# Turning keys, queries and values of the Delta heads and values of GLA in 32x32 blocks through DRAM, and moving beta into the decays

## Chip, cores and metric

One Trainium2 chip, one NeuronCore of it. The metric is device microseconds of one execution. The kernel before has a median of 978.31 us over three runs (978.17 to 978.34). The profile is one execution whose span, first to last instruction, is 976.7 us.

## What is computed

One inference step of two layers over 256 prompt tokens and 8 x 8 sample tokens, width 2048. Layer 0 mixes tokens with 8 gated Delta heads (128 x 128) and 4 GLA heads (128 x 256), layer 1 with an RG-LRU; each has one big projection in and one out. The change touches the two kinds of heads of layer 0. For a Delta head, with keys k and queries q of norm one, G the running sum of the decays and b the beta of a token:

```python
kb = k * beta[..., None]
A = jnp.where(strict, jnp.einsum('nbhid,nbhjd->nbhij', kb, k) * decay, 0.0)
rhs = jnp.concatenate([v * beta[..., None], kb * jnp.exp(G)[..., None]], axis=-1)
sol = lax.linalg.triangular_solve(A + jnp.eye(C, dtype=jnp.float32), rhs,
                                  left_side=True, lower=True, unit_diagonal=True)
qk = jnp.einsum('nbhid,nbhjd->nbhij', q, k) * decay
# per chunk, state S:
v_new = u_c - w_c @ S;  o = qg_c @ S + qk_c @ v_new
S = S * exp(g_last) + k_dec.T @ v_new
```

GLA needs, per chunk, the products of its scores and of its decayed keys with its values v.

## The kernel before

**The main stream.** The weights are cut into 30 groups of 512 columns with 8 chunks of 512 KB each. For a chunk TensorE (PE) runs 24 matmuls into acc (L380), each over 320 tokens: two rows of 128 inputs, four blocks of 128 columns, and three products, since weights and activations are split into a high and a low part (wh, wl; xh, xl). SP loads a chunk into one of three buffers wst (L212); ScalarE (ACT) makes wh (L246) and VectorE (DVE) wl (L247), six buffers of each, so three chunks. PE never leaves this stream by itself.

**The background.** All other work are Python generators, advanced one step per slot; a slot comes after each three acc matmuls. The table WAITS gives the number of slots that a generator lets pass at a named point. What results is one fixed order of instructions per engine; no engine reorders at run time. SP issues its DMAs in order too and has eight rotating lanes: a DMA waits until the DMA eight places ahead on its lane has landed. A wait of any instruction therefore holds all that stands behind it on its engine.

**Delta heads.** The projection leaves k, q and v with the head's dimension on partitions and tokens along the row. delta_half(0) and delta_half(1) each treat four heads over 256 tokens, as two quads (c = 0 and 1: four heads, 128 tokens); delta_sample treats the sample tokens as one more quad. In quad_a (L710) TensorE transposes k (kt, L716), q (qt, L725) and v (vt, L767) of the four heads; ACT copies the turned keys and squares keys and queries for the norms; the decays' matrix dtm comes from df (L751), gr from the same; kk (L773) times dtm is bt, kq (L785) times dtm is mt. nb is minus beta over the squared key norm; it is turned too (nbt, L795) and stored by POOL to nb_scratch. bt's diagonal 32 x 32 blocks go by SP to bd_scratch (L780).

**The inverse.** invert32 (L806) loads the blocks of eight heads' units with four DMAs into ab (L817) and nb into bn (L819), POOL multiplies the two (L823), runs 31 steps of two operations (L828, L830) and stores the inverse blocks to xd_scratch (L835). load_inv (L867) loads them as XT (L871) and, in other places, xc (L876). quad_front (L896) transposes xc into xz on DVE (L910, L920), multiplies blocks on PE (lp, L916; lxt, L926), and DVE scales lp by nb into xp (L907), which the next lxt reads. quad_b then makes y0, the outputs and the state. The sample's inverse runs on DVE (L838).

**GLA.** gla_head, per head and chunk, transposes two blocks of values (gvt, L1438) and the decayed keys (L1439) on PE; ACT copies the three.

Of the kernel before, what the change touches and what calls it, by code (L numbers as in the profile page):

```python
# [7 lines left out]
F32 = mybir.dt.float32  # L8
# [6 lines left out]
P = 128  # L15
# [57 lines left out]
def hybrid_step(ctx, tc, x_cols, x_rows, w_head, w_dense, w_small, w_lr, w_gate, par_a, par_b, par_c, gains, last_gain,  # L73
# [9 lines left out]
    nb_d = nc.dram_tensor("nb_scratch", (20, P), F32, kind="Internal").ap()  # L83
# [3 lines left out]
    xt_d = nc.dram_tensor("xt_scratch", (4, P, P), F32, kind="Internal").ap()  # L87

# [457 lines left out]

    def evac_conv_a(slot_name, half, part):
# [133 lines left out]
    def quad_prompt(half, c):  # L681
# [10 lines left out]
        q.late = c > 0  # L692
        q.on_tag, q.nbuf = "lg", 2
        return q

    def quad_sample():
# [9 lines left out]
        q.late = True  # L706
        q.on_tag, q.nbuf = "bt", 1
        return q

    def quad_a(q, ws, nbuf):  # L710
        U = q.U
        t = lambda nm, shape=[P, 4, P], bufs=nbuf, tag=None: ws.tile(shape, F32, name=nm, tag=tag or nm, bufs=bufs)
        ss = t("ss", [P, 8])
        ps = bank4("kt")
        for u in range(U):
            pe.transpose(ps[:, u, :], q.k(u), ident)  # L716
        q.ktm = t("ktm")
        act.activation(q.ktm, ps, AF.Copy)
        for u in range(U):
            j = t("junk", [P, P], 1)  # L720
            act.activation(j, ps[:, u, :], AF.Square, accum_out=ss[:, u:u + 1])
        yield from wait("quad_a.1")
        ps = bank4("qt")
        for u in range(U):
            pe.transpose(ps[:, u, :], q.q(u), ident)  # L725
        for u in range(U):
            j = t("junk", [P, P], 1)
            act.activation(j, ps[:, u, :], AF.Square, accum_out=ss[:, 4 + u:5 + u])
        q.bk = t("bk", [P, 4])
        q.nb = t("nb", [P, 4])  # L730
        q.nbe = t("nbe", [P, 4])
        sk = ss[:, 0:4]
        pool.tensor_scalar(sk, sk, EPS, None, op0=OP.add)
        pool.tensor_tensor(q.bk, sk, mhalf[:, :4], OP.pow)
        pool.tensor_mul(q.bk, q.bk, beta[:, q.gc:q.gc + 4])
# [8 lines left out]
        yield from wait("quad_a.2")  # L744
        dve.reciprocal(q.nb, sk)
        dve.scalar_tensor_tensor(q.nb, q.nb, -1.0, beta[:, q.gc:q.gc + 4], op0=OP.mult, op1=OP.mult)
# [13 lines left out]
        dve.tensor_mul(dt, dt, q.um[:, None, :].to_broadcast([P, 4, P]))  # L760
        q.eq = ss[:, 4:8]
        dve.tensor_scalar(q.eq, q.eq, EPS, EPS * P, op0=OP.add, op1=OP.mult)
        dve.tensor_mul(q.nbe, q.nb, es[:, q.gc:q.gc + 4])
        yield from wait("quad_a.3")
        ps = bank4("vt")
        for u in range(U):
            pe.transpose(ps[:, u, :], q.v(u), ident)  # L767
        q.rv = t("rv")
        scaled4(q.rv, ps, q.bk, NA0)
        yield from wait("quad_a.4")  # L770
# [5 lines left out]
        yield from wait("quad_a.5")  # L776
# [18 lines left out]
        pe.transpose(ps[:4, :P], q.nb, ident)  # L795
        nbt = t("nbt", [4, P], 1)
        act.activation(nbt, ps[:4, :P], AF.Copy)
        pool.dma_start(nb_d[q.id:q.id + 4, :], nbt)
        yield from wait("quad_a.7")
# [6 lines left out]
    def invert32(ws, first):  # L806
# [4 lines left out]
        bn = ws.tile([P, n], F32, name="bn", tag="bn")  # L811
# [7 lines left out]
        act.dma_start(bn, bass.AP(tensor=nb_d.tensor, offset=nb_d.offset + first * P, ap=[[0, 4], [n, 4 * U], [1, n]]))  # L819
# [3 lines left out]
        pool.tensor_mul(ab, ab, bn[:, None, :].to_broadcast([P, n, n]))  # L823
# [14 lines left out]
    def invert(ws, n_units, n):  # L838
# [4 lines left out]
        bn = ws.tile([parts, n], F32, name="bn", tag="bn")  # L843
# [5 lines left out]
        act.dma_start(bn[:parts], nb_d[16:16 + n_units].rearrange("u (b i) -> (u b) i", i=n))  # L849
# [3 lines left out]
        dve.tensor_mul(ab[:parts], ab[:parts], bn[:parts, None, :].to_broadcast([parts, n, n]))  # L853
# [42 lines left out]
    def quad_front(qs, x, x2, pt, xt, xc):  # L896
# [8 lines left out]
        def scale(ps, rows, w):  # L905
            for c, q in enumerate(qs):
                dve.tensor_mul(pt[c][rows, :, :w], ps[rows, 4 * c:4 * c + 4, :w],  # L907
# [1190 lines left out]
```

## Time and profile before

| what | value |
|---|---|
| median of three runs | 978.31 us |
| span of the profiled execution | 976.7 us |
| PE busy | 965.7 us (99%) |
| DVE, ACT, POOL busy | 695.6, 532.6, 193.4 us |
| granted TensorE clock, mean | 0.997 |
| busy share of the DMA queue of SP (q1) | 54.5% |
| packets under 512 B of all | 17116 of 68125 |
| half 0's quads, first kk to first lp on PE | 122.30 to 193.00 us |
| half 1's | 239.80 to 310.35 us |

The profiled execution has only its span; the runs' times are about 1.6 us above it. In rows of a timeline the columns are start, duration, engine, line, operation and tiles; "x4" means that several are shown as one row, whose duration runs from the first's start to the last's end. In the list of waits the columns are total, count and longest. A matmul's recorded duration is longer than its distance to the next, because PE pipelines them. SPq is SP's queue: its durations are those of issuing, not of the transfer.

### The profile page before, as it was taken

The page shows a single profiled execution, that of the slowest core. Times are in us where ns is not written, and L with a number is a line of the kernel's source. Part 1 is how long each engine was busy: PE and PEld are TensorE (multiplying, and loading weights), DVE is VectorE, ACT ScalarE, POOL GpSimd, SP SyncE. Part 2 cuts the span into 40 slices and gives each one's busy share as a digit, 9 for nine tenths or more (in the row PEclk, how much of TensorE's full clock was granted, in tenths as well). Part 3 has the DMA queues.
Part 4 walks back from the last instruction along what each step waited for, and adds up shares of the span by engine and source line. Part 5 has one row for each costly group of instructions (what it writes and reads, how often), then busy time and mean ns, then how long its engine had stood idle before and what let it go on. Part 6 is the DMA issues. An engine that isn't in the chain of part 4 may idle for free.

```text
span 976.7 us, 18827 instructions
## 1 busy us (share of the span) xinstructions
PE 965.7 (99%) x6945; PEld 949.2 (97%) x6945; DVE 695.6 (71%) x1464; ACT 532.6 (55%) x1088; POOL 193.4 (20%) x343
## 2 busy tenths in 40 slices
PE   9999999999999999999999999999999999999996
PEld 9999999999999999999989999999999999999996
DVE  7498887666545556788658789667969668876763
ACT  7666865447333454866423345348685885333442
POOL 3010128303381011120106124100010000042200
PEclk9999999999999999999999999999999999999998
DMA  9854445534455376444578887655445445678752
GB/s 321 292 176 123 134 131 155 166 109 121 150 154 150 98 235 215 130 125 130 180 251 265 245 246 249 211 154 151 157 117 189 131 127 171 189 229 253 264 168 108
DMA packets 68125, 175.06 MB, mean 179 GB/s; under 512 B 17116, under 2 KB 26096, under 8 KB 67520
## 3 DMA queue, kind: packets, MB, share of 16 engines
q1 hardware_dynamic: 62904, 163.69, 54.5%
q0 software_dynamic: 2720, 8.66, 2.5%
q10 hardware_dynamic: 2408, 1.49, 0.5%
q8 instruction: 55, 0.90, 0.4%
q14 instruction: 38, 0.31, 0.1%
HBM read 159.14 MB, written 14.68 MB: 178 GB/s over the span
## 4 chain that ended last, share of the span: by engine, by line
PE 96%; DVE 2%; issue 0%; DMA 0%; ACT 0%; SPq 0%; POOL 0%; DVEq 0%; ACTq 0%; POOLq 0%
PE acc L380 82%; PE acc L266 3%; PE fbt L309 1%; PE gpo L1495 0%; PE lg L1683 0%; PE lg L1682 0%; PE lg L1684 0%; PE kq L785 0%; PE kk L773 0%; DMA wst<-in_w_head_dram 0%; PE gsn L1259 0%; PE po L971 0%; PE pq L1059 0%; PE sn L1245 0%; PE y L962 0%
## 5 line engine op out<-in xcount | busy, mean ns | idle before, releaser
L380 PE MATMUL acc<-xh,wh 128*128 128x320 f32 x1856 | 579.9, 313 | 0.4 <-ACT wh L233 0.4
L380 PE MATMUL acc<-xl,wh 128*128 128x320 f32 x1856 | 574.0, 310 | 0.0
L380 PE MATMUL acc<-xh,wl 128*128 128x320 f32 x1856 | 573.0, 309 | 0.2 <-DVE wl L247 0.2
L246 ACT ACTIVATE wh<-wst 128x512 fp32r<-128x512 f32 x479 | 279.2, 624 | 301.1 <-PE acc L380 259.5
L247 DVE TENSOR_TENSOR wl<-wst,wh 128x512 fp32r<-128x512 f32 x479 | 333.4, 726 | 150.6 <-ACT wh L246 149.6
L380 PEld LDWEIGHTS acc<-xh,wh 128*128 128x128 f32 x1856 | 348.6, 188 | 3.3 <-issue 1.3
L380 PEld LDWEIGHTS acc<-xl,wh 128*128 128x128 f32 x1856 | 348.6, 188 | 1.1
L380 PEld LDWEIGHTS acc<-xh,wl 128*128 128x128 f32 x1856 | 348.2, 188 | 0.9 <-DVE wl L247 0.4
L588 DVE SCALAR_TENSOR_TENSOR yc<-slab,pa,yc 128x344 f32<-128x344 f32 x72 | 40.6, 576 | 2.8 <-ACT yc L102 2.4
L830 POOL TENSOR_TENSOR xi<-xi,tmp 128x60 f32<-128x60 f32 (+24 forms) x62 | 25.9, 418 | 4.9
L828 POOL TENSOR_TENSOR tmp<-ab,xi 128x60 f32<-128x60 f32 (+24 forms) x62 | 25.1, 404 | 4.8
L1711 POOL MEMSET aa<- 128x32 f32 x4 | 0.6, 161 | 117.7 <-ACT rr L1698 66.7
L1140 POOL TENSOR_TENSOR uvkh<-uvk,uvkh 32x256 fp32r<-32x256 f32 (+1 forms) x8 | 10.8, 1344 | 51.5 <-DVE uvkh L1136 50.6
L1249 DVE SCALAR_TENSOR_TENSOR ust<-ust,es,sn 128x128 f32<-128x128 f32 x64 | 18.2, 338 | 2.8 <-PE sn L1245 2.0
L1145 POOL TENSOR_TENSOR uvm<-uvh,rm 96x512 fp32r<-96x512 f32 x16 | 19.5, 1242 | 2.8 <-PE sn L1245 2.4
L885 POOL TENSOR_TENSOR so<-so,mhalf 128x4 f32<-128x4 f32 x4 | 4.4, 1106 | 74.2 <-DVE so L884 74.2
L266 PE MATMUL acc<-xl,wh 128*128 128x320 f32 (+1 forms) x64 | 18.7, 292 | 0.0
L266 PE MATMUL acc<-xh,wl 128*128 128x320 f32 (+1 forms) x64 | 18.7, 292 | 0.0
L266 PE MATMUL acc<-xh,wh 128*128 128x320 f32 (+1 forms) x64 | 18.6, 291 | 0.0
L592 ACT ACTIVATE qkv<-yc 128x256 f32<-128x256 f32 x24 | 10.0, 415 | 15.8 <-DVE yc L588 15.6
L1263 DVE SCALAR_TENSOR_TENSOR ugt<-ugt,ebs,gsn 128x256 f32<-128x256 f32 x32 | 14.1, 474 | 5.6 <-PE gsn L1259 5.5
L1642 DVE SCALAR_TENSOR_TENSOR yc<-slab,pb,yc 128x344 f32<-128x344 f32 x32 | 17.5, 572 | 0.6 <-ACT yc L1640 0.5
(464 smaller groups left out, 1057.1 us busy)
## 6 DMA issues: line engine op xcount, KB each, us to landing
wst<-in_w_dense_dram SPq DMA_DIRECT2D x237, 512.0 KB, 4.0
st<-in_state_delta_dram SPq DMA_DIRECT2D x8, 512.0 KB, 6.3
st<-in_state_gla_dram SPq DMA_DIRECT2D x4, 1024.0 KB, 6.9
ust<-in_state_delta_dram SPq DMA_DIRECT2D x8, 512.0 KB
out_s_delta_dram<-ust POOLq DMA_DIRECT2D x8, 512.0 KB, 5.1
ugt<-in_state_gla_dram SPq DMA_DIRECT2D x8, 512.0 KB, 5.6
out_s_gla_dram<-ugt POOLq DMA_DIRECT2D x8, 512.0 KB, 4.2
xtok<-in_x_rows_dram SPq DMA_DIRECT2D x6, 512.0 KB, 5.4
```

The costliest lines, as they stand in the source:

```text
L246: act.activation(h, wst[i][:, a, :], AF.Copy)
L247: env["last_split"] = dve.tensor_sub(l, wst[i][:, a, :], h.bitcast(F32))
L266: mm = pe.matmul(accs[f][:, cols], w[:, fs], x[:, cols], start=(k == 0 and j == 0), stop=(k == KT - 1 and j == 2), skip_group_check=True)
L380: mm = pe.matmul(o, (h, h, l)[j][:, fs], (xh, xl, xh)[j][k], start=(k == 0 and j == 0), stop=(k == KT - 1 and j == 2))
L588: dve.scalar_tensor_tensor(y[:, :n], xp[:, j:j + n], pa[:, ft, j:j + 1], y[:, :n], op0=OP.mult, op1=OP.add)
L828: behind(pool.tensor_mul(tv, ab[:, j, j + 1:, None].to_broadcast([P, m, w]), xi[:, j:j + 1, :w].to_broadcast([P, m, w])))
L830: behind(pool.tensor_add(xi[:, j + 1:, :w], xi[:, j + 1:, :w], tv))
L1140: pool.tensor_sub(o, t[rows, :, cols], o.bitcast(F32))
L1145: pool.tensor_mul(m, src.bitcast(F32)[:, None, :].to_broadcast([R, 4, P]), rm4[:R, :, None].to_broadcast([R, 4, P]))
L1249: dve.scalar_tensor_tensor(s_, s_, es[:, col:col + 1], ps[:, b, :], op0=OP.mult, op1=OP.add)
L1263: dve.scalar_tensor_tensor(s_, s_, ebs[:, h, 4 * hb + b + i:4 * hb + b + i + 1], ps[:, i * 256:(i + 1) * 256], op0=OP.mult, op1=OP.add)
L1642: dve.scalar_tensor_tensor(y[:, :n], xp[:, j:j + n], pb[:, ft, 2 + j:3 + j], y[:, :n], op0=OP.mult, op1=OP.add)
```

## The change

The turn is no longer made on PE. As soon as a column group has left k, q or v, turn (new) has DVE transpose its 32 x 32 blocks into a buffer of the layer (ob) and SP store that to tp_scratch (512 KB; 256 KB to ts_scratch for the sample). quad_a then loads each tensor with four strided DMAs of 128 x 128 (load_turned), which put the blocks where the whole transpose would have them: kin, qin and rv for kt, qt and vt. Which of the tensors is loaded late depends on the half (late): in half 0 the values, in half 1 the queries. GLA's values go the same way; its keys stay on PE. In the loaded values the 32-column blocks of a head are apart, so y0's and GLA's matmuls and some DVE operations read them in strides.

The rows of bt are scaled by nb while it is made: dtm is multiplied by nb and the mask in one operation per head. So nbt, its store, bn and POOL's multiplication of ab go, and lp is only copied into xp, by DVE for one quad and ACT for the other. v, eg and wv use other factors accordingly. quad_a's waits are moved, and quad_a.7 falls from 9 slots to 2.

```diff
-    "quad_a.4": 0, "quad_a.5": 0, "quad_a.6": 0, "quad_a.7": 9, "invert32.1": 18, "invert32.2": 13,
+    "quad_a.4": 0, "quad_a.5": 0, "quad_a.6": 0, "quad_a.7": 2, "invert32.1": 18, "invert32.2": 13,
...
+    def turn(src, d, flag, to, gate):
+        while gate not in env["done"]:
+            yield
...
+        for f in range(4):
+            behind(dve.transpose(out[:, f], src[:, f, :].rearrange("p (x j) -> p x j", j=32)))
+            yield from wait("turn.1")
+        yield from wait("turn.2")
+        behind(sp.dma_start(d, to))
+        env["done"].add(flag)
+        yield from wait("turn.3")
+
+    def load_turned(out, d, c=0):
+        w = d.shape[1]
+        for b in range(4):
+            sp.dma_start(out[32 * b:32 * b + 32].rearrange("p a u j -> p a (u j)"), bass.AP(
+                tensor=d.tensor, offset=d.offset + c * 4 * P + b * P, ap=[[w, 32], [32 * w, 4], [1, P]]))
...
     def quad_a(q, ws, nbuf):
-        ps = bank4("kt")
-        for u in range(U):
-            pe.transpose(ps[:, u, :], q.k(u), ident)
...
+        kin = rows("kin", "mt")
+        load_turned(kin, *turned(1))
+        late = {0: 2, 1: 0}.get(half)
+        if late != 0:
+            qin = rows("qin", "bt")
+            load_turned(qin, *turned(0))
+        if late != 2:
+            q.rv = rows("rv")
+            load_turned(q.rv, *turned(2))
...
-        dve.tensor_mul(dt, dt, q.um[:, None, :].to_broadcast([P, 4, P]))
...
+        for u in range(U):
+            j = t("junk", [P, P], 1)
+            act.activation(j, q.ktm[:, u, :], AF.Square, accum_out=ss[:, u:u + 1])
...
+        for u in range(U):
+            dve.scalar_tensor_tensor(dt[:, u, :], dt[:, u, :], q.nb[:, u:u + 1], q.um, op0=OP.mult, op1=OP.mult)
...
-        ps = bank("nbt")
-        pe.transpose(ps[:4, :P], q.nb, ident)
...
     def invert32(ws, first):
-        pool.tensor_mul(ab, ab, bn[:, None, :].to_broadcast([P, n, n]))
...
     def quad_front(qs, x, x2, pt, xt, xc):
-        def scale(ps, rows, w):
-            for c, q in enumerate(qs):
-                dve.tensor_mul(pt[c][rows, :, :w], ps[rows, 4 * c:4 * c + 4, :w],
-                               q.nb[rows, :, None].to_broadcast([rows.stop - rows.start, 4, w]))
+        def keep(ps, rows, w):
+            dve.tensor_copy(pt[0][rows, :, :w], ps[rows, 0:4, :w])
+            act.activation(pt[1][rows, :, :w], ps[rows, 4:8, :w], AF.Copy)
...
     def gla_head(h, ws, vt):
-            for hf in range(2):
-                pe.transpose(pt[:, hf, :], env["VB", vt // 4][:, vt % 4, cs], ident)
```

On PE the products of both quads of a half now stand in one block: kk, kq, kk, kq. In half 0 they come behind 744 acc matmuls (before: 726 and 730) and lp behind 1134 (before 1171); in half 1 behind 1350 (1383 and 1387) and 1740 (1827). Half 0 thus has 390 acc matmuls between the products and lp, where 441 stood between the second quad's products and lp; half 1 has 390 too, where 440 stood.

SP in half 0, from the blocks' stores on; bd_scratch are bt's diagonal blocks, ab their load for the inverse, wst a chunk of weights. Before:

```order
L780 DMA bd_scratch<-bt 32x4x32 x8
L212 DMA wst<-in_w_dense_dram 128x1024
L817 DMA ab<-bd_scratch 32x1024 x2
L520 DMA out_dconv_dram<-stc 128x108
L817 DMA ab<-bd_scratch 32x1024
L212 DMA wst<-in_w_dense_dram 128x1024
L817 DMA ab<-bd_scratch 32x1024
L212 DMA wst<-in_w_dense_dram 128x1024 x7
```

And after the change, where tp_scratch is the store of the turned values and rv their loads:

```order
L213 DMA wst<-in_w_dense_dram 128x1024 x3
L830 DMA bd_scratch<-bt 32x4x32 x8
L561 DMA tp_scratch<-ob_137 128x1024
L213 DMA wst<-in_w_dense_dram 128x1024
L880 DMA ab<-bd_scratch 32x1024
L569 DMA rv<-tp_scratch 32x4x128 x8
L880 DMA ab<-bd_scratch 32x1024 x3
L213 DMA wst<-in_w_dense_dram 128x1024 x2
L521 DMA out_dconv_dram<-stc 128x108
```

The eight loads of values and their store now stand between the blocks' stores and three of their four loads, and one chunk stands there, not two.

SP in half 1, before:

```order
L212 DMA wst<-in_w_dense_dram 128x1024 x10
L780 DMA bd_scratch<-bt 32x4x32 x8
L212 DMA wst<-in_w_dense_dram 128x1024
L817 DMA ab<-bd_scratch 32x1024
L212 DMA wst<-in_w_dense_dram 128x1024
L817 DMA ab<-bd_scratch 32x1024 x2
L212 DMA wst<-in_w_dense_dram 128x1024
L817 DMA ab<-bd_scratch 32x1024
```

and after, from the loads of the second quad's keys on (kin and qin are turned keys and queries):

```order
L569 DMA kin<-tp_scratch 32x4x128 x4
L569 DMA rv<-tp_scratch 32x4x128 x4
L213 DMA wst<-in_w_dense_dram 128x1024
L561 DMA tp_scratch<-ob_137 128x1024
L830 DMA bd_scratch<-bt 32x4x32 x8
L569 DMA qin<-tp_scratch 32x4x128 x4
L213 DMA wst<-in_w_dense_dram 128x1024 x2
L569 DMA qin<-tp_scratch 32x4x128 x4
L561 DMA ts_scratch<-ob_139 128x512
L213 DMA wst<-in_w_dense_dram 128x1024
L880 DMA ab<-bd_scratch 32x1024 x4
```

Between the blocks' stores and the first of their loads stand now eight loads of queries, a store of the sample's turned tensor and three chunks; a burst of sixteen loads (keys and values of two quads) stands ahead of one more chunk.

DVE where half 0's inverse comes back: xz are its blocks, turned from xc; xp is what the first lp leaves for lxt. Before:

```order
L247 TENSOR_TENSOR wl<-wst,wh 128x512
L588 SCALAR_TENSOR_TENSOR yc<-slab,pa,yc 128x344
L910 STREAM_TRANSPOSE xz<-xc 32x8x32 x2
L588 SCALAR_TENSOR_TENSOR yc<-slab,pa,yc 128x344
L247 TENSOR_TENSOR wl<-wst,wh 128x512
L588 SCALAR_TENSOR_TENSOR yc<-slab,pa,yc 128x344
L907 TENSOR_TENSOR xp<-lp,nb 32x4x32
L588 SCALAR_TENSOR_TENSOR yc<-slab,pa,yc 128x344
L907 TENSOR_TENSOR xp<-lp,nb 32x4x32 x3
```

and after, where ob are the sample's keys being turned:

```order
L967 STREAM_TRANSPOSE xz<-xc 32x8x32 x2
L977 STREAM_TRANSPOSE xz<-xc 32x8x32
L558 STREAM_TRANSPOSE ob_139<-smpK 128x4x32
L248 TENSOR_TENSOR wl<-wst,wh 128x512
L558 STREAM_TRANSPOSE ob_139<-smpK 128x4x32
L248 TENSOR_TENSOR wl<-wst,wh 128x512
L480 TENSOR_TENSOR slab<-acc,rb_84 128x256
L481 TENSOR_TENSOR slab<-acc,rb_84 128x8x8
L964 COPY xp<-lp 32x4x32
```

The first copy of lp now stands behind two more splits (wl) and two evacuations of acc into slab; before one split stood there.

More of the change, by code (lines that the diff above doesn't have):

```diff
@@ L606, in after @@
                 hi.append(later(lambda: lo.extend([delta_half(1), delta_sample()])))
+            if part or half:
+                turn_conv(part, half, ob[1], "x0")
+            if part == 1 and half == 0:
+                turn_conv(0, 0, ob[0], "x0")
+            if half:
+                turn_sample(part)
         evac.late = late
@@ L692, in quad_prompt @@
         q.late = c > 0
+        q.at = half, c
         q.on_tag, q.nbuf = "lg", 2
@@ L712, in quad_a @@
         t = lambda nm, shape=[P, 4, P], bufs=nbuf, tag=None: ws.tile(shape, F32, name=nm, tag=tag or nm, bufs=bufs)
+        half, c = q.at
+        turned = lambda part: (tp_d[2 * part + half], c) if q.n == 32 else (ts_d[part], 0)
         ss = t("ss", [P, 8])
-        ps = bank4("kt")
-        for u in range(U):
[L716 to L735, printed above, removed]
+        rows = lambda nm, tag=None: t(nm, [P, 4, 4, 32], tag=tag)
+        kin = rows("kin", "mt")
[7 more added lines that the diff above has]
+            load_turned(q.rv, *turned(2))
         if q.n == 32:
@@ L743, in quad_a @@
                            g.bitcast(F32)[:, q.gc:q.gc + 4, None].to_broadcast([P, 4, P]))
-        yield from wait("quad_a.2")
-        dve.reciprocal(q.nb, sk)
-        dve.scalar_tensor_tensor(q.nb, q.nb, -1.0, beta[:, q.gc:q.gc + 4], op0=OP.mult, op1=OP.mult)
+        q.bk = t("bk", [P, 4])
+        q.nb = t("nb", [P, 4])
+        q.nw = t("nw", [P, 4])
+        q.eq = ss[:, 4:8]
+        sk = ss[:, 0:4]
+        yield from wait("quad_a.1")
         def summed(mask, nm):
@@ L775, in quad_a @@
         dve.tensor_mul(q.bt, ps, dt)
-        yield from wait("quad_a.5")
+        yield from wait("quad_a.4")
         if q.n == 32:
@@ L789, in quad_a, with rest @@
         else:
-            half = lambda x, e: x.rearrange("p u (q e x) -> p (u q) e x", e=2, x=16)[:, :, e, :]
+            side = lambda x, e: x.rearrange("p u (q e x) -> p (u q) e x", e=2, x=16)[:, :, e, :]
             for e in range(2):
-                dve.tensor_mul(half(q.mt, e), half(ps, e), half(dt, 1 - e))
+                dve.tensor_mul(side(q.mt, e), side(ps, e), side(dt, 1 - e))
         yield from wait("quad_a.6")
-        ps = bank("nbt")
[L795 to L799, printed above, removed]
+        w0 = 20 + q.gc if q.n == 32 else 36
+        dve.tensor_mul(q.nw, q.nb, es[:, w0:w0 + 4])
+        if late != 2:
+            v_scale()
+        def rest():
+            while ("t", late, half) not in env["done"]:
+                yield
+            x = rows("rv") if late else rows("qin", "pt")
+            load_turned(x, *turned(late))
+            yield from wait("quad_a.8")
+            if late:
+                q.rv = x
+                v_scale()
+            else:
+                q_sums(x)
+            env["done"].add(("rows", q.id))
+        if late is not None:
+            lo2.append(rest())
     def diag_ap(d, first, n_units, n):
@@ L1008, in delta_half @@
             yield from wait("quad_b.1")
+            for q in qs:
+                while ("rows", q.id) not in env["done"]:
+                    yield
             yield from quad_front(qs, z[:, :, :64], z[:, :, 64:], pt, xt, xc)
@@ L1028, in load @@
                     sp.dma_start(st[:, e], state_delta[2 * u + e])
+            front = quad_a(q, ws, 1)
+            next(front)
+            yield
             load(0)
             load(1)
-            yield from quad_a(q, ws, 1)
+            yield from front
             yield from invert(ws, 4, 8)
@@ L1434, in gla_head @@
                 act.activation(at[ks, qs], ps[ks, i, a:a + n], AF.Copy)
[L1435 to L1441 removed]
+            pt = bank("gvt")
+            pe.transpose(pt[:, :P], kd[128][:, cs], ident)
+            vk = t("gvk", [P, P])
+            act.activation(vk, pt[:, :P], AF.Copy)
             yield from wait("gla.3")
             po = bank("gpo")
[L1444 to L1445 removed]
+            split = lambda x: x[:, :256].rearrange("p (f a j) -> p f a j", f=2, j=32)
+            vtm = vt[c][:, :, 2 * (h % 2):2 * (h % 2) + 2, :].rearrange("p a f j -> p f a j")
+            pe.matmul(split(po), at, vtm, start=True, stop=not c)
             if c:
@@ L1448, in gla_head @@
             ps = bank("gsn")
-            pe.matmul(ps[:, :256], vk[:, 2, :], vtm, start=True, stop=True)
+            pe.matmul(split(ps), vk, vtm, start=True, stop=True)
             if c == 0:
@@ L1462, in gla @@
             for h in (0, 2):
-                yield from weave(gla_head(h, ws), gla_head(h + 1, ws))
+                while ("t", "VB", h // 2) not in env["done"]:
+                    yield
+                vt = [ws.tile([P, 4, 4, 32], F32, name="gvv", tag="gvv", bufs=4) for _ in range(2)]
+                for c in range(2):
+                    load_turned(vt[c], tp_d[6 + h // 2], c)
+                yield from weave(gla_head(h, ws, vt), gla_head(h + 1, ws, vt))
         with tc.tile_pool(name="glas", bufs=1, side="right", reuse_waits="tile") as ws:
```

86 lines of the change are left out of this document (49 added, 37 removed), and 4 rows, old and new, of the table WAITS.

## The prediction

> **What bounds the kernel now.** I read the page first (busy shares, the chain that ended last), then the list of TensorE's waits, then the timelines of PE, SP, POOL and DVE around the Delta heads' inverse. The page's busy row and its chain:
>
> ```profile
> PE 965.7 (99%) x6945; PEld 949.2 (97%) x6945; DVE 695.6 (71%) x1464; ACT 532.6 (55%) x1088; POOL 193.4 (20%) x343
> PE 96%; DVE 2%; issue 0%; DMA 0%; ACT 0%; SPq 0%; POOL 0%; DVEq 0%; ACTq 0%; POOLq 0%
> ```
>
> All that PE waits for, in total:
>
> ```profile
> PE frs L352 <- DVE rr L350: 1.4, 1, 1.4
> PE got L1306 <- DVE gon L1302: 1.2, 2, 0.6
> PE warm L1833 <- DVE mhalf L1821: 1.1, 1, 1.1
> PE acc L380 <- ACT wh L233: 0.4, 1, 0.4
> PE acc L380 <- DVE wl L247: 0.2, 1, 0.2
> ```
>
> PE is 99% busy and waits 4.3 us of 976.7. So every matmul that goes is a gain in full, and every wait that comes is a loss in full: there is no slack on PE to absorb either. The span is 976.7 and the median of the runs 978.31, so 1.6 us lie around it; I sum on the span and add 1.6.
>
> **What goes from PE.** A group of four transposes between main matmuls, and the groups by tile:
>
> ```profile
> 110.72 0.31 PE L380 MATMUL acc<-xh,wl 128*128 128x320 f32 x1
> 110.88 0.60 PE L716 MATMUL kt<-ident,qkv 128*128 128x128 f32 x4
> 111.23 0.39 PE L380 MATMUL acc<-xh,wh 128*128 128x320 f32 x1
> 111.46 0.31 PE L380 MATMUL acc<-xl,wh 128*128 128x320 f32 x1
> ...
> L716 PE MATMUL kt<-ident,qkv x16: 270/272/273, 110.9 to 229.6; 128*128 128x128 f32 x16
> L716 PE MATMUL kt<-ident,smpK x4: 272/272/273, 345.6 to 345.9; 128*128 128x128 f32 x4
> L795 PE MATMUL nbt<-ident,nb x5: 272/272/273, 124.1 to 354.0; 128*4 128x128 f32 x5
> L1438 PE MATMUL gvt<-ident,gp x16: 272/276/281, 416.0 to 473.8; 128*128 128x128 f32 x16
> ```
>
> The main matmuls' spacing comes from this group, 441 of them between the first quads' products and the inverse's use:
>
> ```profile
> L380 PE MATMUL acc<-xl,wh x147: 308/309/392, 128.1 to 192.5; 128*128 128x320 f32 x147
> L380 PE MATMUL acc<-xh,wl x147: 307/309/309, 128.4 to 192.6; 128*128 128x320 f32 x147
> L380 PE MATMUL acc<-xh,wh x147: 309/309/309, 128.5 to 192.8; 128*128 128x320 f32 x147
> ```
>
> 441 starts span 64.7 us (128.1 to 192.8): 0.147 us each, though a record lasts 309 ns. With no transposes the matmul at 111.46 would start two spacings after 110.72, at 111.02; the four cost 0.44 us, 0.11 each. qt and vt stand as often as kt: 5 quads x 3 x 0.44 = 6.6. The 16 value transposes of GLA: 16 x 0.11 = 1.8. Five nbt, by the step from 124.09 to the next main matmul at 124.12, 0.03 each: 0.1. The gain is 8.5 us.
>
> By the records' durations it would be 81 x 0.272 = 22 us. The Trainium skill ("TensorE: Matmul & The Clock Gate", Part 4: PE-mode transpose) gives about 275 ns for one in a kernel's context: the trace agrees on the duration, but starts 0.11 us apart say that this is no price per transpose here; by the page the time would be 13 us lower.
>
> **What is added beside PE.** Nearest rows for the new DVE, ACT and SP work (three multiplications and a stream transpose of DVE; the split of a weight; a weight's landing; a 512 KB store; a small SP DMA):
>
> ```profile
> 127.33 0.42 DVE L111 TENSOR_TENSOR rv<-vt,bk 128x256 f32<-128x256 f32 x1
> 127.66 0.68 DVE L775 TENSOR_TENSOR bt<-kk,dtm 128x512 f32<-128x512 f32 x1
> ...
> 192.37 0.89 DVE L910 STREAM_TRANSPOSE xz<-xc 32x256 f32<-32x256 f32 x2
> ...
> 195.00 0.28 DVE L907 TENSOR_TENSOR xp<-lp,nb 32x128 f32<-32x128 f32 x1
> ...
> L246 ACT ACTIVATE wh<-wst 128x512 fp32r<-128x512 f32 x479 | 279.2, 624 | 301.1 <-PE acc L380 259.5
> L247 DVE TENSOR_TENSOR wl<-wst,wh 128x512 fp32r<-128x512 f32 x479 | 333.4, 726 | 150.6 <-ACT wh L246 149.6
> ...
> wst<-in_w_dense_dram SPq DMA_DIRECT2D x237, 512.0 KB, 4.0
> out_s_delta_dram<-ust POOLq DMA_DIRECT2D x8, 512.0 KB, 5.1
> ...
> 128.37 1.73 SPq L780 DMA_DIRECT2D bd_scratch<-bt  x4
> ```
>
> DVE gets 32 block transposes 128x256 and 12 of 128x128. The row has 0.43 us for 32x256; at the same time per column 32 x 0.43 + 12 x 0.22 = 16 us, and four times that if partitions counted. Beside DVE's idle 29% the low end hides, and I take it: DVE's products of 512 and 256 columns on 128 partitions and of 128 columns on 32 (0.68, 0.42, 0.28) lie on one line, so partitions do not count there. The Trainium skill speaks against the move ("VectorE: DVE Perf Modes", The three transpose paths and Rules for kernel authors): VectorE turns 32x32 blocks only, and a 128x128 transpose belongs on TensorE. Nothing in before runs DVE as a whole-tile transpose; the rest of the turn is what the DMAs below pay.
>
> SP gets 11 stores (8 of 512 KB) and 76 more small loads, at 0.43 each (the bd row: 1.73 for four) 33 us of SP's time, in bursts of 8 and 16 between weight loads. SP's queue is in order, so each burst delays the weight behind it. A weight must be issued some 5 us before its use (4.0 landing, then wh's 0.62); PE's 0.2 us of waits for wl say that it has been so far, a burst of eight costs 3.4 us, and I cost this at nothing outside the two places below, and at up to 2 us in the sample's and GLA's stretches. The beta scaling that leaves POOL and DVE only moves small work there.
>
> **The two places: the inverse.** kk makes bt; bt's blocks go through DRAM to POOL, which inverts them, back through DRAM, transposed by DVE, and then PE's lp uses them. Half 0, then half 1:
>
> ```profile
> 122.30 1.06 PE L773 MATMUL kk<-qkv 128*128 128x128 f32 x8
> 123.19 1.06 PE L785 MATMUL kq<-qkv 128*128 128x128 f32 x8
> ...
> 193.00 0.25 PE L916 MATMUL lp<-xz,bt 128*32 128x32 f32 x2
> ...
> 239.80 1.06 PE L773 MATMUL kk<-qkv 128*128 128x128 f32 x8
> ...
> 310.35 0.70 PE L916 MATMUL lp<-xz,bt 128*32 128x32 f32 x32
> ```
>
> SP's last load of the blocks (ab) and last load of the inverse (xc), and POOL's beta multiplication, of both halves:
>
> ```profile
> 137.64 0.43 SPq L817 DMA_DIRECT2D ab<-bd_scratch  x1
> 187.03 0.43 SPq L876 DMA_DIRECT2D xc<-xd_scratch  x1
> 255.49 0.44 SPq L817 DMA_DIRECT2D ab<-bd_scratch  x1
> 303.12 0.43 SPq L876 DMA_DIRECT2D xc<-xd_scratch  x1
> ...
> 142.02 2.56 POOL L823 TENSOR_TENSOR ab<-ab,bn 128x1024 f32<-128x1024 f32 x1 [12.10 <-DVE wl L247]
> 144.66 0.56 POOL L828 TENSOR_TENSOR tmp<-ab,xi 128x31 f32<-128x31 f32 x1
> ...
> 260.68 2.40 POOL L823 TENSOR_TENSOR ab<-ab,bn 128x1024 f32<-128x1024 f32 x1 [13.62 <-PE acc L380]
> ```
>
> I count from the start of the first kk. *PE's side.* Before, lp stood 70.7 (half 0) and 70.6 us behind it. The changed order puts all four products of a half together, 4 x 0.89 (122.30 to 123.19) = 3.6 us, and then only 390 main matmuls, 57.2 us: lp is due after 60.8 us, 9.8 earlier. *The chain's side, before.* Half 0: the last ab issue came at 15.3, the last xc issue 49.4 later; a landing like a store's 1.8 us (an estimate: the bd blocks' ab loads follow them that fast) and the transposes' 0.9 make 67.4. It was 3.3 us early. Half 1: 15.7 + 47.6 + 2.7 = 66.0, 4.6 early. *After.* The multiplication goes: -2.6 (142.02 to 144.66). With the same front the chain ends at 64.8 and 63.4, that is 4.0 and 2.6 us after PE is due. So the front, from kk to the last ab issue, decides.
>
> Half 0's front: the second bt comes earlier, since its kk starts 1.8 behind the first: with its 0.9, DVE's 0.7 and 0.3 between them, at 3.7; its blocks' four stores end at 5.5; then the store of the turned values, a weight, one ab load, and eight loads of the values, the first of which waits till that store has landed, and behind these the other three ab loads. With a landing of 4.5 (between 1.8 of a small store and 5.1) the values' loads run from 10.3 to 13.8, and the last ab issue is at 14.6 (11.5 to 16.5). Stall at lp: 14.6 + 49.4 - 2.6 + 2.7 - 60.8 = 3.3 (0 to 5). Then the next use: a weight is queued on SP behind the xc loads, its split stands on DVE ahead of the copy xp, and lxt, 15 matmuls (2.2 us) behind lp, needs xp. From the xc issue: 0.5 + 4.0 + 2 x 0.62 + 0.73 + about 1 = 7.5, against lp's 2.7 + 0.8 + 2.2: 1.8 us (0 to 3). Half 0: 5.
>
> Half 1's front: bt now needs beta and the norms ahead of it (its mask is scaled by nb), and these need the keys' loads, which stand on SP in a burst of 16, 6.9 us of issue; the squares stand on ACT behind the split of the same chunk. I put the second bt at 8 (between 3.7, as in half 0, and 10). Behind it on SP: four stores, four loads, two weights, four loads, a store, a weight, and only then the four ab loads: 8.7 + 8 = 16.7 without any wait for a transfer, 18.5 with one weight's landing. Stall: 18.5 + 47.6 - 2.4 + 2.7 - 60.8 = 5.6 (0.8 to 8), and another 1 (0 to 2) at lxt: 6.6. The weight in that queue falls inside it: it is late by the same lateness of bt, ahead of lp.
>
> Sum: 976.7 - 8.5 + 5 + 6.6 + 1.6 = 981.4. The unknowns' ends: 0.8 us of stalls give 970.6, and 18 with 2 for the later stretches 989.8.
>
> **Rivals.** *The waits hide* (chance 0.26): the turned stores land as fast as small ones and the second bt of half 1 is as early as in half 0. Below a front of 11.3 us in half 0 and of 12.9 in half 1 no stall is left at lp. Then the stalls are 0 to 6 us and the time 969.8 to 976. For it: 3 to 5 us of slack were there, and 2.6 us go from the chain. Against: PE's side lost 9.8.
> *Stalls eat the gain* (0.22): 6.5 to 10.5 us of stalls, 976.3 to 980.3, about 978: one half behaves, the other as forecast.
> *Half clock behind each stall* (0.06, on the slower side): if the granted clock fell to half for as long as the stall behind it (half 0's 3.3 and half 1's 5.6, say 9 us at half speed), 4.5 us more: 986. Before's mean clock is 0.997, and it has no wait over 1.4 us, so no row bears on it. The Trainium skill has such a rule ("TensorE: Matmul & The Clock Gate", Why this matters for your kernels: no idle gap over about 3 us), and no run here shows it.
> *DVE becomes the bound* (within the slower chance): at four times the price the transposes cost 64 us of DVE, which its idle 281 us (976.7 - 695.6) hold on the whole; but they stand between splits, at 1.7 us each, and where three follow each other a split comes 5 us late: perhaps 5 us in all, 986, and waits for wl would show it.
> *It doesn't do what it says*: the values stay strided in 32-column blocks, and if the matmuls that read them ran slower (16 y0, 16 gpo and gsn), at most doubled records, it is under 2 us.
>
> **The numbers.** Forecast with its own range 980.3 to 987, chance 0.46, and the half clock's 0.06: slower 0.52. Same 0.22, faster 0.26; 0.2% is 2 us, about what a measurement tells from no change. The range, 970 to 989, takes in the clean case and leaves out less than 1 in 10 on the upper side.
>
> **What would show it.** Right: no transposes of kt, qt, vt and nbt; PE's waits list names lp (for xz) and lxt (for xp) with 2 to 6 us each; lp about 64 us behind kk in half 0 and 67 in half 1; xc's loads end just before. Wrong: lp due at 61 us and no wait there (then the front was shorter than 11 us), or long waits at acc for wl outside these places (then SP's bursts or DVE are the cost), or PE's groups not 8.5 us shorter.

## The result and the profile after

The changed kernel takes 992.12 us in the median of four runs (990.75 to 994.25), beside 978.24 us of the kernel before on the same chip (977.65 to 978.34): ratio 1.0143, 95% interval 1.0131 to 1.0156. It is slower by 13.9 us, the sign that was forecast, but 4.5 times the 3.1 us of the forecast; the time lies above the range. The profiled execution has a span of 989.3 us.

Busy time, from the page of the changed kernel:

```profile
PE 965.2 (98%) x6864; PEld 946.3 (96%) x6864; DVE 707.9 (72%) x1521; ACT 523.2 (53%) x1073; POOL 184.8 (19%) x336
```

PE has 81 instructions less and as much busy time as before (965.7). What PE waits for, in total, times, longest:

```profile
PE lp L973 <- DVE xz L967: 4.7, 4, 2.3
PE lxt L983 <- issue: 3.3, 1, 3.3
PE got L1374 <- DVE gon L1370: 2.3, 3, 1.0
PE acc L381 <- ACT wh L247: 1.9, 1, 1.9
PE y L1020 <- DVE rv L1012: 1.4, 2, 1.1
PE frs L353 <- DVE rr L351: 1.4, 1, 1.4
PE df L786 <- DVE ug L774: 1.3, 1, 1.3
PE warm L1902 <- DVE mhalf L1890: 1.1, 1, 1.1
PE ot L1167 <- DVE on L1162: 0.8, 1, 0.8
PE acc L381 <- ACT wh L234: 0.3, 1, 0.3
```

They sum to 18.5 us, before to 4.3: 14.2 more. lp, lxt and a weight (wh) stand at the two places of the forecast. "issue" beside lxt means that the list names nobody whom it waited for; experiment 6 shows the rows. But the waits are not all. The windows of the changed kernel (columns: busy us and count of PE, PEld, DVE, ACT, POOL, then the granted clock PEclk, the DMA share and GB/s) around lxt in half 0, the late weight and lp in half 1:

```profile
192.00:194.00 2.00, 0.00 (x0) 0.00 (x0) 1.84 (x7) 1.10 (x3) 0.00 (x0) 0.95 0.79 225
194.00:196.00 2.00, 1.85 (x50) 1.79 (x51) 1.97 (x6) 1.80 (x5) 0.00 (x0) 0.50 0.68 256
196.00:198.00 2.00, 2.00 (x11) 2.00 (x11) 1.43 (x4) 1.13 (x3) 0.00 (x0) 0.70 0.23 79
...
258.00:260.00 2.00, 1.85 (x8) 1.86 (x9) 1.29 (x2) 1.15 (x3) 0.00 (x0) 0.66 1.16 305
260.00:262.00 2.00, 2.00 (x9) 2.00 (x9) 1.29 (x2) 1.91 (x9) 0.00 (x0) 0.50 1.08 330
...
306.00:308.00 2.00, 0.49 (x11) 0.38 (x13) 1.95 (x6) 0.00 (x0) 0.00 (x0) 0.61 0.94 348
308.00:310.00 2.00, 2.00 (x35) 1.94 (x31) 1.52 (x5) 0.27 (x1) 0.00 (x0) 0.50 0.26 107
310.00:312.00 2.00, 2.00 (x11) 1.67 (x10) 1.14 (x3) 0.64 (x2) 0.00 (x0) 0.50 0.39 106
312.00:314.00 2.00, 2.00 (x53) 1.62 (x53) 1.38 (x3) 1.21 (x3) 0.00 (x0) 0.68 0.42 164
```

Behind each of three waits the granted clock is 0.50, and main matmuls start 0.267 us apart, not 0.147: a slow spell, as it is called from here on. A window of 2 us at a granted share of 0.50 misses 1 us of clock. Summed over the windows, 1.7, 1.7 and 3.4 us are missing, so the spells last 3.4, 3.4 and 6.8 us. Of the 6.8 us that are missing, some 0.8 fall into waits (0.35 us of the wait at lxt and 1.24 us of the second one at lp lie inside a spell), so the matmuls lost about 6.

The sum of the two traces: 989.3 - 976.7 = 12.6. PE's groups without their waits are 8.4 us shorter (2.8 around the products, 4.3 at the turned keys and queries, 1.3 at GLA's values). Waits add 14.2, and 12.6 + 8.4 - 14.2 = 6.8 are left: the slow spells, and what the list leaves out of the waits. It counts a wait from the end of a main matmul's record (0.31 us), and the next start was due 0.147 us after the last; so each wait costs some 0.16 us more than it is listed with. That is an estimate; for the ten more waits it makes 1.6 us, which would leave 5 to 7 us for the spells. The median of the runs lies 2.8 us above the profile's span, before 1.6.

### The profile page after: what moved, and what is told of

Read it like the earlier page. It is cut to its first block, busy times and chain, and to the rows that moved or that the text cites. A ratio compares the mean times of both kernels' runs of the same rounds, so it can differ in the third digit from the quotient of the medians.

```text
span 989.3 us, 18826 instructions
## 1 busy us (share of the span) xinstructions
PE 965.2 (98%) x6864; PEld 946.3 (96%) x6864; DVE 707.9 (72%) x1521; ACT 523.2 (53%) x1073; POOL 184.8 (19%) x336
## 4 chain that ended last, share of the span: by engine, by line
PE 69%; POOL 3%; DMA 2%; DVE 2%; SPq 1%; issue 1%; ACT 1%; DVEq 0%; POOLq 0%; ACTq 0%
PE acc L381 58%; PE acc L267 3%; POOL xi L891 1%; POOL tmp L889 1%; PE fbt L310 1%; DMA wst<-in_w_dense_dram 1%; DMA ab<-bd_scratch 0%; PE lg L1752 0%; PE lg L1751 0%; PE lg L1753 0%; PE pq L1124 0%; PE gsn L1325 0%; PE sn L1311 0%; PE ga L1495 0%; SPq L929 0%
## 5 line engine op out<-in xcount | busy, mean ns | idle before, releaser
L103 ACT ACTIVATE yc<-slab,pa 128x344 f32<-128x344 f32 x24 | 13.7, 577 | 8.3 <-DVE slab L481 7.5
```

Of the source, the lines that this page charges most:

```text
L103: return act.activation(out, in_, AF.Identity, scale=scale)
```

## The experiments

All ratios are against the kernel before, run on the same chip; its median there was 978.9 to 979.3 us. Theory A is the one of the sum above: PE's waits around the inverse, with a slow spell behind each long one. Its main rival B: the turn's load on DVE and SP costs by itself, wherever it stands. A' is A without the place of lp; C, D and E say what they are where they come up.

**1. lp later.** WAITS alone:

```diff
-"quad_b.1": 23
+"quad_b.1": 37
```

> The changed kernel with one number altered: quad_b.1 of 37 slots, not 23, so that lp and all that follows it stand 42 main matmuls (6.2 us) later behind kk. Theory A (the loss is TensorE's waits where it reaches the inverse too early, with a spell of slow matmuls behind each long wait): the waits at lp (4.7), lxt (3.3) and y (1.4) go, 9.4 us, and about 3 us of slow matmuls behind them; the wait of 1.9 at a weight in half 1 and the slow spell behind it stay: 992.1 - 12.5 = 979.6. Theory B (the turn itself loads DVE, SP and the strided operands): at most 2 us better, 990 or more.

Measured 989.87 us, ratio 1.0106 (1.0087 to 1.0126). The waits at lp are gone and those at lxt down to 1.0, but in half 0 the wait is now at a main matmul, for the evacuation of the group before it:

```profile
PE acc L381 <- DVE slab L481: 3.9, 1, 3.9
PE acc L381 <- ACT wh L247: 2.3, 1, 2.3
```

A misses by 10 us. B's "990 or more" is met within the spread of the runs (988.98 to 991.61), so this run does not rule B out. Where lp stands decides who waits, and little of how long: PE's waits sum to 18.1 us, beside 18.5. (The wait quad_a.7, whose number the change lowers, is no longer called in the changed quad_a; lp's place comes from the order as a whole.)

**2. The kernel before, with lp early.** Its turns stay on TensorE; shorter waits, and the next main matmul is ordered behind lp:

```diff
-"invert32.2": 13, "invert32.5": 8
+"invert32.2": 0, "invert32.5": 6
+        env["first"] = lp
...
+                    if "first" in env:
+                        tc.add_manual_dep(mm.ins, env.pop("first").ins.name, ...)
```

> The kernel before, with all its turns on TensorE, but with shorter waits (invert32.2 0 for 13, invert32.5 6 for 8) and the main matmuls held behind lp, so that lp stands 46 main matmuls (6.8 us) earlier behind kk. From its slack of 3.3 and 4.6 us: waits at lp of 3.7 us in half 0 and 2.1 in half 1. Theory A with slow spells: after a wait of 2 us or more main matmuls start 0.267 us apart for 3 to 4 us, which costs 1.5 us each: 978.3 + 5.8 + 3 = 987. If slow spells belong to the turned loads and not to the wait: 984, and spacing stays at 0.147. Theory B (place of lp without weight): 978 to 979.

Measured 992.04 us, ratio 1.0127 (1.0107 to 1.0147). Its wait at lp, and the windows behind it in half 0:

```profile
PE lp L919 <- DVE xz L913: 6.5, 4, 3.0
...
192.00:194.00 2.00, 2.00 (x28) 1.94 (x24) 1.89 (x7) 0.87 (x2) 0.00 (x0) 0.50 1.07 354
194.00:196.00 2.00, 2.00 (x53) 1.60 (x52) 1.11 (x2) 0.41 (x2) 0.00 (x0) 0.50 0.50 201
```

Waits of 6.5 us at lp (5.8 expected) cost 12.9 us, 5 more than A has, with no turned load in the kernel. Over both halves 5.1 us of clock are missing, counted by windows as above, where 3 us were expected; with the 7.6 us by which all of PE's waits grew that is 12.7. So the slow spells belong to the wait, and waits with their spells cost not quite twice the waits (7.6 and 12.9 us).

**3. Late loads behind the inverse's blocks.** lp at the change's place; in both halves the late loads come behind the four ab loads, and half 1's scaling of the values with them:

```diff
         def rest():
-            while ("t", late, half) not in env["done"]:
+            while ("t", late, half) not in env["done"] or ("ab", half) not in env["done"]:
                 yield
+            if late == 0:
+                v_scale()
```

> The changed kernel, lp at its place, but in both halves the late loads (values in half 0, queries in half 1) are issued only behind the four ab loads, and half 1's scaling of the values comes behind them too. Theory A: the last ab issue comes about 4 us earlier in half 0 (13.3 us behind the first kk now) and 5 to 6 in half 1 (20.9 now), the weight behind the queries' loads comes in time; the waits at lp (4.7), lxt (3.3) and at the weight (1.9) go, and 4.5 us of slow matmuls: 977 to 980. If only lp's place matters and not SP's order: 989 or more. Theory B: 990 or more.

Measured 987.46 us, ratio 1.0079 (1.0059 to 1.0098). A's 977 to 980 and B's 990 are both missed. The wait for wh goes and that at lp falls from 4.7 to 2.0, but lxt keeps 3.4. SP's order ahead of the inverse is a part of the loss (by the ratios, 0.0064 of 979, 6 us), and not all.

**4. Both.**

> Both edits together: the late loads behind the ab loads, and lp 42 main matmuls later. Theory A: no wait at lp, lxt, y or a weight is left, no slow spell, and the 8.4 us of transposes that went from TensorE show: 978.3 - 8.4 + 2.5 (waits at df and got, 2.3 over before's) = 972. Theory B: 985 or more.

Measured 982.95 us, ratio 1.0039 (1.0027 to 1.0050). A's 972 is missed by 11 us, and B's 985 by 2. lp, lxt and the weight in half 1 cost 0.4 us together; a wait of 2.9 for slab stays in half 0, with a slow spell.

**5. Is it DVE's place?** As 4, with DVE's transposes of the inverse held behind the main matmuls beside which they stand in the code:

```diff
-            dve.transpose(dst[cut(b)], xc[cut(b)])
+            behind(dve.transpose(dst[cut(b)], xc[cut(b)]))
```

> As front_and_later, and DVE's transposes of the inverse (xz from xc) are held behind the main matmuls beside which they stand in the code, so that in half 0 the splits and the evacuations of acc come ahead of them on DVE. Theory A': the 2.9 us at acc for slab in half 0, with a slow spell of 1.5 us, came from DVE standing at xz for the xc transfer with these behind it: 982.9 - 4.4 = 978.5. If the weight, queued on SP behind the xc loads, is late by itself: the wait stays as one for wl or wh, 982 or more.

Measured 985.32 us, ratio 1.0062 (1.0047 to 1.0077): no gain, the wait for slab is 2.2 us. Here DVE's timeline of half 0 has no transpose ahead of the split any more, and DVE waits all the same, for ACT's part of a weight:

```profile
189.44 0.69 DVE L248 TENSOR_TENSOR wl<-wst,wh 128x512 fp32r<-128x512 f32 x1 [5.33 <-ACT wh L247]
```

The evacuations stand behind this split. So the weight is late by itself. With lp some 21 main matmuls earlier (quad_b.1 at 30) it is no better:

> As xz_behind with quad_b.1 at 30 slots, so lp stands 18 to 21 main matmuls earlier than there and the later heads less late. Theory A: lp is due 63.5 us behind the first kk; with the front of front_shorter the chain needs about 61.5 in half 0 and 63 in half 1: no wait over 1 us at lp; 978 to 980. If a wait of over 2 us comes at lp or lxt: 983 or more.

Measured 986.40 us, ratio 1.0077 (1.0055 to 1.0099): waits of 2.7 for slab and 1.3 at lxt, and a spell.

**6. The weight behind the inverse's loads.** SP in half 0 of the changed kernel:

```profile
164.06 9.21 SPq L213 DMA_DIRECT2D wst<-in_w_dense_dram  x4
179.41 2.72 SPq L929 DMA_DIRECT2D XT<-xd_scratch  x4
182.18 0.44 SPq L934 DMA_DIRECT2D xc<-xd_scratch  x1
182.66 1.93 SPq L929 DMA_DIRECT2D XT<-xd_scratch  x4
184.63 0.43 SPq L934 DMA_DIRECT2D xc<-xd_scratch  x1
185.16 0.45 SPq L213 DMA_DIRECT2D wst<-in_w_dense_dram  x1
...
190.14 1.15 ACT L247 ACTIVATE wh<-wst 128x512 fp32r<-128x512 f32 x2 [7.57 <-DMA wst<-in_w_dense_dram]
...
190.80 0.69 DVE L248 TENSOR_TENSOR wl<-wst,wh 128x512 fp32r<-128x512 f32 x1 [2.31 <-ACT wh L247]
...
193.75 0.30 DVE L964 COPY xp<-lp 32x128 f32<-32x128 f32 x1
```

After a weight at 173.3 us SP issues nothing till 179.41: the next in its queue are the inverse's loads, and POOL issues the inverse's stores from 175.5 to 178.1. The weight behind them goes out at 185.16, and ACT stood 7.57 us for it. DVE's split waits for ACT's part, and the copies xp that lxt reads stand behind the split; lxt starts at 194.15. In the order before the change these loads stand behind two more weights in half 0, and behind three more in half 1. Put back by two, first with the change's other loads as they are, then with 3's edit:

```diff
-"delta_half.1": 0
+"delta_half.1": 14
-                sp.dma_start(q.xt[bs, :, bs], ...)
+                behind(sp.dma_start(q.xt[bs, :, bs], ...))
-        sp.dma_start(q.xc, ...)
+        behind(sp.dma_start(q.xc, ...))
```

> lp_later (lp 42 main matmuls later in half 0, 42 in half 1), by 14 slots in front of the loads of the inverse (delta_half.1) in place of behind them, and these loads held at that place in SP's order: they stand two weights further back in SP's queue than in the change, as they did before it. Theory E (a weight is late because it is queued on SP behind the inverse's loads, which stand there until POOL has stored the inverse): the wait of 3.9 at acc in half 0 and the slow spell behind it go: 989.9 - 5.5 = 984. If the wait at acc belonged to DVE's order or to the turn's other loads: 989 or more.

> inv_loads_behind with the late loads behind the ab loads (as in front_shorter and front_and_later). Theory E: front_and_later's wait of 2.9 at acc and the slow spell behind it go, 982.9 - 4.5 = 978.4, the time before the change. Otherwise 982 or more.

Measured 985.19 us, ratio 1.0058 (1.0037 to 1.0078), and 981.26 us, ratio 1.0021 (1.0011 to 1.0032). Theory E has 984 and 978.4: the first comes within 1.2 us, the second is missed by 2.9. The wait for slab and the spell behind it in half 0 are gone in both; the first keeps one wait of 3.4 us at a weight in half 1, which the second has not. The second has no spell at all, clock 0.998. Its longest waits:

```profile
PE ot L1170 <- DVE on L1165: 2.4, 2, 1.3
PE lxt L986 <- issue: 2.1, 2, 1.1
```

Of the change's 13.9 us, 2.0 are left. What holds them are waits of 1.3 us and less, 13.4 us in all against 4.3, which eat the 8.4 us of transposes. These figures give a loss of 0.7 us, and the profiled span is 2.6 longer than before's; the 0.16 us that the list leaves out of each wait, for nine more waits, would be 1.5 of the rest (an estimate).

**7. The turn added and not used.** The kernel before, all its transposes on TensorE, and the whole turn beside them (GLA's values only turned and stored):

> The kernel before with the whole turn added and unused: DVE's block transposes, the stores, and the strided loads of the Delta heads' k, q and v into tiles that nobody reads (GLA's values are turned and stored, and not loaded). All transposes stay on TensorE, lp stands 441 main matmuls behind the products as before. Theory A: in place of slack the ab loads come 4 us later, which eats most of 3.3 and 4.6 us: waits of 0 to 2 us at lp and about as much at weights, 980 to 984. Theory B (DVE and SP load is itself the cost): 988 or more.

Measured 997.48 us, ratio 1.0199 (1.0175 to 1.0224). A's number is missed by 13 us: it is as slow as B has it. Yet most of the loss is made of waits, 13.6 us of them over before's in the profiled execution, whose span is 16.2 us longer. SP's last loads ahead of the inverse in half 0, and PE's longest waits:

```profile
135.04 1.73 SPq L570 DMA_DIRECT2D lin<-tp_scratch  x4
...
142.14 3.21 SPq L570 DMA_DIRECT2D lin<-tp_scratch  x3
...
146.39 2.04 SPq L877 DMA_DIRECT2D ab<-bd_scratch  x4
...
PE lxt L986 <- issue: 5.2, 2, 2.8
PE lp L976 <- DVE xz L970: 2.8, 4, 1.3
```

The last ab load goes out 21.1 us behind the first kk (126.86 to 148.0), where it was 15.3 before and 19 was expected. In half 1 it is 21.4 (247.86 to 269.25), where it was 15.7. So ahead of the inverse the load of the turn acts through SP's queue, and lp's early place is not needed for the loss; that the waits at lxt come from a weight queued there, as in 6, was not tested in this kernel. B's "wherever it stands" does not hold: the second kernel of 6 has the same turn in another order and loses 2.0 us.

**8. The parts.** beta alone: dtm scaled by nb, no nbt, bn or multiplication on POOL, lp copied; everything else as before.

```diff
-        dve.tensor_mul(dt, dt, q.um[:, None, :].to_broadcast([P, 4, P]))
+        for u in range(U):
+            dve.scalar_tensor_tensor(dt[:, u, :], dt[:, u, :], q.nb[:, u:u + 1], q.um, op0=OP.mult, op1=OP.mult)
...
-        pe.transpose(ps[:4, :P], q.nb, ident)
...
-        pool.tensor_mul(ab, ab, bn[:, None, :].to_broadcast([P, n, n]))
```

> The kernel before with the beta part alone: dtm is scaled by nb per head, no nbt, no bn, no multiplication of ab on POOL, lp copied; all turns stay on TensorE. kk to lp is 441 and 438 main matmuls as before. Theory A: TensorE loses 0.1 us, the chain gets 2.5 us shorter behind 3.3 and 4.6 us of slack: no change, 978.5 to 979.5 beside before's 979.2. If bt comes late because nb must be there first (rival C): waits at lp, 981 or more.

Measured 976.84 us, ratio 0.9978 (0.9969 to 0.9988), 2 us faster than expected; PE's groups around the products are 0.9 us shorter, so nbt cost 0.2 each, not 0.03. The rest of the 2 us is not accounted for. No wait comes at lp, so C (bt late, since nb must be there first) is out here, and nothing new waits for more than 0.3 us:

```profile
PE got L1297 <- DVE gon L1293: 1.5, 3, 0.6
PE frs L352 <- DVE rr L350: 1.4, 1, 1.4
PE warm L1824 <- DVE mhalf L1812: 1.1, 1, 1.1
```

With GLA's values turned too, the Delta heads on TensorE:

> beta_alone with GLA's values turned through DRAM as in the change; the Delta heads' keys, queries and values stay on TensorE. 16 transposes go (1.3 us by the sums over TensorE's groups). Theory A' (the cost of the turn is the lateness of loads that somebody waits for, and GLA's values have time between their group and gla_head): 976.8 - 1.3 = 975.5, no new wait over 0.5 us. Theory B (the turn's load costs wherever it stands): 978 or more.

Measured 977.19 us, ratio 0.9982 (0.9973 to 0.9991): PE's groups are shorter by the 1.3 us, a wait of 0.6 comes at gvt, and the time is that of beta alone within the interval. A' is missed by 1.7 us: no gain of turning GLA's values shows, and B's 978 is not reached either. The change without GLA's part:

> The changed kernel with GLA's values back on TensorE: the Delta heads' turn and the beta part remain. Theory A': all the loss is the Delta heads', so 992.1 + 1.3 = 993.4 (991 to 995). If GLA's loads and stores had a share in the loss: 990 or less.

Measured 994.24 us, ratio 1.0155 (1.0140 to 1.0169), within the 991 to 995 expected. The loss is the Delta heads'.

**9. What of the Delta heads can be turned.** As 8 with GLA, and the prompt's queries and values turned, both loaded behind the ab loads; keys and the sample's heads on TensorE (32 transposes go):

```diff
+        def rest():
+            for f in (("t", 0, half), ("t", 2, half), ("ab", half)):
+                while f not in env["done"]:
+                    yield
+            q.rv = t("rv", [P, 4, 4, 32])
+            load_turned(q.rv, tp_d[4 + half], c)
...
+            load_turned(x, tp_d[half], c)
```

> beta_and_gla, and of the prompt's Delta heads the queries and the values too, loaded after the ab loads; their keys and the sample's heads stay on TensorE. Nothing ahead of the inverse waits for a turned tensor. 32 + ... 16 transposes of queries and 16 of values go, 3.5 us. Theory A': 975.5 - 3.5 = 972, with up to 2 us given back where SP's bursts stand ahead of a weight: 972 to 974. Theory B, or if the chain through the ab loads still gets later than its slack: 978 or more, with waits at lp or lxt.

Measured 976.38 us, ratio 0.9965 (0.9953 to 0.9978): faster than the kernel before by 2.9 us, where 7 were expected. Some 2 of the 2.9 are there with beta alone; the two intervals overlap, so the runs do not show that turning queries and values gains anything, only that it costs nothing that shows. lp and lxt wait for nothing. The span is 973.5, and the largest new wait is elsewhere:

```profile
PE gvt L1539 <- POOL gvs L1538: 1.8, 1, 1.8
```

And the keys as well, loaded at the quad's start and used 8 slots later:

> late_qv with the prompt's keys turned through DRAM too, loaded at the start of the quad and used 8 slots later; only the sample's heads keep their turns on TensorE. 16 more transposes go, 1.8 us. kk stands 43 to 78 main matmuls later than in late_qv, and lp 427 to 445 behind it, as far as before the change. Theory A' (only loads that come late ahead of the inverse cost, the turn as such does not): 976.4 - 1.8 = 974.6, waits at lp and lxt under 1 us. Theory D (the keys are what cannot be turned this way, since bt now waits for their norms): waits of 2 us or more behind kk, 980 or more.

Measured 984.00 us, ratio 1.0046 (1.0033 to 1.0060). Above 980 as theory D has it, but not by its wait: behind kk, lxt waits 0.9 and lp nothing. The later work of the heads stands up to 66 main matmuls later, and the waits are there, with two slow spells behind them:

```profile
PE y L1134 <- DMA XT<-xt_scratch: 3.0, 1, 3.0
PE gvt L1550 <- POOL gvs L1549: 2.8, 1, 2.8
```

So time given to the keys ahead of the inverse seems to be taken from the sample's heads and GLA; no run moves these back to show it.

## Why the prediction was wrong

*What goes from PE*: 8.5 us forecast, 8.4 measured. The price per transpose was right; that the sum fits so well is partly luck, as GLA's values gave 1.3 where 1.8 were put and the five nbt 0.9 where 0.1 was. The page of the Trainium skill that gives 275 ns for a transpose ("TensorE: Matmul & The Clock Gate", Part 4: PE-mode transpose) agrees with the records; at that price 81 transposes would have given 22 us. The distance of starts was the price.

*Half 0*: 5 us forecast (3.3 at lp, 1.8 at lxt), 4.5 measured (1.2 and 3.3). The sum is near because two errors cancel. The front was 13.3 us, from kk at 125.44 to the last ab issue, beside 14.6. The weight queued behind the inverse's loads was named for lxt and sized too small. It reaches further than lxt: in experiments 1, 4 and 5 a main matmul waits for the evacuation behind the same split.

*Half 1*: 6.6 us forecast, 5.5 measured (1.9 at the weight, 3.6 at lp, none at lxt). The front was 20.9 us, not 18.5, and by the forecast's own sum that is 8.0 at lp. It was less because the inverse took 43.4 us from the last ab issue to the last xc issue, where 45.2 were put, and PE itself came later by its wait at the weight and the spell behind it. So the near sum is luck here too. DVE holds the second bt behind the scaling of the values, which waits for POOL. DVE in half 1, SP behind it, and ACT:

```profile
244.58 0.16 DVE L810 TENSOR_SCALAR ss<-ss 128x4 f32<-128x4 f32 x1
...
246.86 0.69 DVE L809 TENSOR_TENSOR rv<-rv,bk 128x512 f32<-128x512 f32 x1 [1.44 <-POOL bk L817]
...
249.09 0.65 DVE L825 TENSOR_TENSOR bt<-kk,dtm 128x512 f32<-128x512 f32 x1
...
251.59 1.81 SPq L569 DMA_DIRECT2D qin<-tp_scratch  x4
253.44 0.91 SPq L213 DMA_DIRECT2D wst<-in_w_dense_dram  x2
...
257.43 3.21 SPq L880 DMA_DIRECT2D ab<-bd_scratch  x4
...
255.40 0.31 ACT L805 ACTIVATE junk<-qin 128x128 f32<-128x128 f32 x1 [9.07 <-DMA qin<-tp_scratch]
...
257.46 1.15 ACT L247 ACTIVATE wh<-wst 128x512 fp32r<-128x512 f32 x2 [0.36 <-DMA wst<-in_w_dense_dram]
```

The second bt starts 9.7 us behind the first kk (8 was taken, 10 the upper end). PE stood 1.9 us for the weight of 253.44. Its late landing is only a part of that: ACT had stood 9.07 us for the queries, whose squares are ahead of the split in its order, and then only 0.36 us for the weight. The forecast named the weight, took it to fall inside the wait at lp, and left out the slow spell behind it.

*Half clock behind each stall*: the step that failed. The forecast's sum put the clock behind a wait at nothing. It stood as a rival with a chance of 0.06, since before has no wait over 1.4 us to show it, and at 4.5 us, with half clock for as long as the stall. Measured are spells of 3.4, 3.4 and 6.8 us, 6.8 us of missing clock, of which the matmuls lost 5 to 7. With 6.8 in the sum, 981.4 would have been 988. Experiment 2 shows the spells without the turn. The rule of the Trainium skill ("TensorE: Matmul & The Clock Gate", Why this matters for your kernels: no idle gap of TensorE over about 3 us between bursts) points the right way. The traces differ on the length: waits of 1.9 us here and of 2.2 in experiment 5 had a spell behind them.

*Outside the two places*: 0 in the sum, and up to 2 allowed in the later stretches; the waits at df (1.3), y (1.4), ot (0.8) and got (1.1 over before) are 4.6. With the slow spells alone the forecast would still have been 4 us short.

From 981.4: 1.6 less at the two places, 4.6 of small waits, 6.8 of slow matmuls and of what the list leaves out of the waits, 1.2 as the runs lie further above the profile than before: 992.4, measured 992.1.

*The rivals.* "The waits hide" fell with the first trace. DVE did not become the bound: a block transpose of 128x256 took 0.44 us, as taken:

```profile
L558 DVE STREAM_TRANSPOSE ob<-qkv x24: 398/436/446, 82.7 to 232.1; 128x256 f32<-128x256 f32 x24
```

The strided operands cost PE 0.2 us at GLA's products. The clean case, 969.8, was not reached by any experiment; the nearest, late_qv, leaves a part of the work on TensorE. What stays open is 1 us of beta's gain.

## What to carry to other kernels

On a TensorE that is 99% busy, count a removed matmul by the distance of starts and not by its duration, and a new wait at up to twice its length from a little under 2 us on. A queue that issues in order passes lateness on: a load that must wait for another engine holds all transfers behind it, so look at what is queued behind each waiting DMA. Moving a turn through DRAM cost nothing that shows where its consumer had time, as for queries and values here, and it did cost for the keys; that it gains is not shown. Moving the consumer later only moves the wait until the queue's order is mended too.

## What the runs showed of the hardware

The granted clock falls to 0.50 behind waits of TensorE of some 2 to 4 us, but not each time; in the changed kernel it stays there for 3.4, 3.4 and 6.8 us. The shortest single wait with a spell right behind it was 1.8 us, at a weight in delta_only (granted share 0.54 from 258 to 260 us), and late_qv has a wait of 1.8 us without one. Short waits close together act alike: in front_shorter, two at lp in half 1, of 0.54 and 1.24 us with ends 1.5 us apart, had a spell behind them:

```profile
306.00:308.00 2.00, 2.00 (x10) 2.00 (x8) 1.52 (x4) 0.30 (x1) 0.00 (x0) 0.50 0.27 63
```

In the unused turn's profiled execution waits of 2.8 us passed without one, as its window behind lxt in half 0 shows:

```profile
206.00:208.00 2.00, 1.91 (x57) 1.90 (x57) 1.97 (x4) 1.56 (x5) 0.00 (x0) 1.00 0.66 200
```

That kernel's runs spread from 994.68 to 1001.17 us, and its profiled run was the fastest of them; before, beta_alone and late_qv, without waits over 1.8 us, spread by 2.3 to 3.7 us. The granted clock of each run fits slow spells that come in some runs and not in others: 0.998 in the run of 994.68 us, 0.995 in that of 996.29, and 0.993 in those of 998.68 and 1001.17. Over some 995 us a share of 0.005 is 5 us of clock. Where in the slower runs it went no trace shows.
